# A two-layer hybrid decoder trunk: layer 0's memory heads in three rounded products of split operands with their maps divided on ScalarE, and layer 1's memory values moved to the end of their slot

## The chip, the cores and the metric

The kernel runs on one core of a Trainium2 chip. The metric is the device time of one execution in microseconds (us); the number compared is the median of several runs. A profile of one execution stands beside it: when each instruction of each engine ran, and what it waited for.

## The reference

Two layers over a sequence of 256 tokens with 2048 channels, in float32, with a memory of 256 further rows. Each layer has a mixer and a squared-ReLU MLP; in both mixers 4 heads attend to the memory:

```python
def memory_cross_attention(q, mem, mem_norm_g, w_mem_kv, mq_g, mk_g):
    mkv = rms_norm(mem, mem_norm_g) @ w_mem_kv
    k = mkv[..., :MEM_WIDTH].reshape(B, M, MEM_HEADS, MEM_HEAD_DIM)      # 256 x 4 x 128
    v = mkv[..., MEM_WIDTH:].reshape(B, M, MEM_HEADS, MEM_HEAD_DIM)
    q = rms_norm(q.reshape(B, S, MEM_HEADS, MEM_HEAD_DIM), mq_g)
    k = rms_norm(k, mk_g)
    s = jnp.einsum('bqhd,bkhd->bhqk', q, k).astype(jnp.float32) * (MEM_HEAD_DIM ** -0.5)
    p = jax.nn.softmax(s, axis=-1).astype(v.dtype)
    return jnp.einsum('bhqk,bkhd->bqhd', p, v).reshape(B, S, MEM_WIDTH)

for i in range(2):
    u = rms_norm(x, mix_norm[i]) @ w_in[i]          # columns 1536.. are the memory queries
    # layer 0: causal pooling over windows 2/4/8/16 and per-group maps; layer 1: differential attention
    x = x + concat([token_out, mem_out]) @ w_out[i]
    x = x + squared_relu_mlp(rms_norm(x, ffn_norm[i]), w_ff1[i], w_ff2[i])
```

A head's map `p` is the exponential of the scores divided by its row's sum.

## The kernel before

**Matrices.** A weight comes from memory in blocks of 128x128, 8 to a load (`raw`, or `slab` for the MLP). ScalarE casts a block to a rounded 32-bit type (`F32R`) into `hi_ring` (L166), and VectorE subtracts that from the original and writes the remainder to `lo_ring` (L169). Activations are split in the same way into a high and a low half. A product of two split operands is then three rounded matmuls (high by high, low by high, high by low) that add up in PSUM; the fourth is left out. Both rings have 6 slots of 4 blocks; casts run up to 3 jobs ahead of their use, and a cast can start only when TensorE has finished with the slot it writes.

**Order.** Each engine runs its instructions in the order in which the program holds them. The program is written as a stream of weight blocks; `tick()` is called after every 4 blocks, and `at(d, fn, rank)` puts a piece of other work `d` ticks later. Within one tick the pieces run by rising rank. A scheduler then settles the final order on each engine, from priorities that follow the written order.

**Layer 0.** The memory's keys and values (`wide_step`, L494: TensorE tiles `mk`, `mv`), the memory queries (`mq`), then the pooling projection in tiles `u` (`a_part`, L463 and L465), 16 blocks each. Between these stand the 4 memory heads. `turn_rows` (L616) transposes keys and queries on TensorE (`tr`) and writes them, times a gain, as plain float32. `mem_head` (L656) is called once per head, 4 ticks apart. It holds three pieces:

- `scores`: two float32 matmuls of 128x256 into `ms` (L663), the row maximum `mm_max` on VectorE (L665), two exponentials on ScalarE (L669) into a buffer of 2x256 columns, their sums kept; 2 ticks later `norm`: a reciprocal `mm_rec` (L676) and two multiplications on VectorE (L678).
- `turn`, 4 ticks after the scores: four transposes of 128x128 into `mt` (L686), copied out by ScalarE (L689).
- `pv`, 8 ticks after: two float32 matmuls of 128x256 into `mo` (L694), in the PSUM bank `o`; ScalarE and VectorE write its two halves to `cat` (L695, L696).

Their ranks are 3, 2 and 1: in a tick that holds all three, an older head's `pv` goes first, then the next head's `turn`, then the newest head's `scores`.

**Layer 1.** The same `mem_head` runs for 4 heads beside 12 heads of differential attention. These use the bank `o` too: their values `do` (L1394 to L1396) go there, and VectorE reads them out as `osb` (L1416). The next matmul into the bank, that of a memory head's `pv`, has to wait for this read. Between the pieces run the tiles `mq` (L476 to L478), then `wo` (L463, L465).

Of the kernel before, what the change touches and what calls it, by code (L numbers as in the profile page):

```python
# [14 lines left out]
ALU = mybir.AluOpType  # L15
# [301 lines left out]
def program(ctx, tc, plan, dry, xT, memT, par, lam, cst, wst, yT):  # L317
# [17 lines left out]
    def at(d, fn, rank=0):  # L335
        pend.setdefault(now[0] + d, []).append((rank, fn))
# [71 lines left out]
    def gcol(c):  # L408
        return param[:, c : c + 1]
# [103 lines left out]
    def columns(name):  # L513

        st = stat("tc_" + name)
        for i in range(2):
            nc.tensor.matmul(
                st[:, 2 * i : 2 * i + 2], acc[name][:, i * P : i * P + P], ones_d[:, 0:2],
                start=True, stop=True,
            )  # L520
        v = cp.tile([P, 2], F32, tag="m2", bufs=12, name="cv")
        nc.vector.tensor_scalar_add(v, st[:, 0:4].rearrange("p (a b) -> p a b", b=2)[:, :, 0], EPS)
        col = cp.tile([P, 2], F32, tag="c_" + name, name="c_" + name)
        rsqrt_cols(col, v)
        col2 = cp.tile([P, 2], F32, tag="d_" + name, name="d_" + name)
        nc.vector.tensor_mul(col2, col, col)
        return col, col2


    def key_rows(ps, cols, d):  # L530

        n = 512 // d
        raw = tp.tile([P, 2, 512], F32, tag="rows", bufs=3, name="krow")
        v = vp.tile([P, 2, n], F32, tag="w16", bufs=6, name="kv")
        for t in range(2):
            nc.scalar.activation(raw[:, t, :], ps[t], AF.Copy, scale=cols[0][:, t : t + 1])
            sq = tp.tile([P, 512], F32, tag="rowsq", bufs=1, name="ksq")
            nc.scalar.activation(sq, raw[:, t, :], AF.Square)
            nc.vector.tensor_reduce(
                out=v[:, t, :], in_=sq.rearrange("p (h d) -> p h d", d=d), axis=AX.X, op=ALU.add  # L540
            )
        v = v.rearrange("p t n -> p (t n)")
        nc.vector.tensor_scalar(out=v, in0=v, scalar1=1.0 / d, scalar2=EPS, op0=ALU.mult, op1=ALU.add)
        y = vp.tile([P, 2 * n], F32, tag="w16", bufs=6, name="ky")
        rsqrt_cols(y, v)
        for t in range(2):
            rows = raw[:, t, :].rearrange("p (h d) -> p h d", d=d)
            yb = y[:, t * n : t * n + n].unsqueeze(2).to_broadcast([P, n, d])
            nc.vector.tensor_mul(rows, rows, yb)
        return raw  # L550
# [66 lines left out]
        nc.scalar.activation(dst, turned(raw, i, tag or ("o" if i else "t")), AF.Copy, scale=g)  # L617


    held = {}  # L620

    def mem_query(src, gq, cols):
# [30 lines left out]
        at(2, stats, -2)  # L653
        return q, y

    def mem_head(q, y, k, v, e, pT, out, lag, tag):  # L656

        def scores():  # L660
            s = bk(tag, "ms", (P, 2, T))
            for t in range(2):
                nc.tensor.matmul(s[:, t, :], q[:, t * P : t * P + P], k, start=True, stop=True)  # L663
            m = cp.tile([P, 2], F32, tag="m2", bufs=12, name="mm_max")
            nc.vector.tensor_reduce(out=m, in_=s, axis=AX.X, op=ALU.max, negate=True)  # L665
            nc.vector.tensor_mul(m, m, y)
            z = cp.tile([P, 2], F32, tag="m2", bufs=12, name="mm_sum")
            for t in range(2):
                nc.scalar.activation(  # L669
                    e[:, t, :], s[:, t, :], AF.Exp, bias=m[:, t : t + 1], scale=y[:, t : t + 1],  # L670
                    accum_out=z[:, t : t + 1],
                )

            def norm():
                zr = cp.tile([P, 2], F32, tag="m2", bufs=12, name="mm_rec")
                nc.vector.reciprocal(zr, z)  # L676
                for t in range(2):
                    nc.vector.tensor_scalar_mul(e[:, t, :], e[:, t, :], zr[:, t : t + 1])  # L678

            at(2, norm)  # L680

        def turn():
            t4 = bk("t", "mt", (P, 2, T))
            for mb in range(2):
                for t in range(2):
                    nc.tensor.transpose(  # L686
                        t4[:, mb, t * P : t * P + P], e[:, t, mb * P : mb * P + P], ident
                    )
            nc.scalar.copy(pT, t4)  # L689

        def pv():
            o = bk("o", "mo", (P, T))
            for mb in range(2):
                nc.tensor.matmul(o, v(mb), pT[:, mb, :], start=mb == 0, stop=mb == 1)  # L694
# [47 lines left out]
    def ffn(l, xs, tags, done):  # L742
# [245 lines left out]


    big = sp.tile([P, 4096], F32, tag="big", name="big0")  # L990
    half = sp.tile([P, 2048], F32, tag="half", name="half0")
# [5 lines left out]
    pTb = big[:, 3264:3776].rearrange("p (a t) -> p a t", a=2)  # L997
    mk = half[:, 0:1024].rearrange("p (h t) -> p h t", h=4)
    ebuf = [
        half[:, 1024 + i * 512 : 1536 + i * 512].rearrange("p (a t) -> p a t", a=2) for i in range(2)  # L1000
    ]
    for u in ups:
        nc.vector.memset(u[:, :, 0:16], 0.0)

# [45 lines left out]
            mem_chunk(1)  # L1050
    two_squares("mem", memraw, NK - 2)
    mem_c.extend(columns("mem"))
    mrow = key_rows(kps, mem_c, P)
    for i in range(2):
        at(8, lambda i=i: turn_rows(mrow, 2 * i, mk[:, 2 * i : 2 * i + 2, :], gcol(G_MK)))
# [33 lines left out]
    mq0 = tp.tile([P, 4, T], F32, tag="rows", bufs=3, name="mq0")  # L1089
    for i in range(2):  # L1090
        at(4, lambda i=i: turn_rows(rows0, 2 * i, mq0[:, 2 * i : 2 * i + 2, :], mqg0))
    for h in range(4):
        mem_head(
            mq0[:, h, :], y0.rearrange("p (t h) -> p t h", t=2)[:, :, h], mk[:, h, :],
            lambda mb, h=h: mv[:, mb, h * P : h * P + P], ebuf[h % 2], pTb, cat[:, 12 + h, :],
            6 + 4 * h, f"n{h % 2}",
        )
    pooled = sp.tile([P, 12, 512], F32R, tag="S1", name="pooled")

    def group_u(g):  # L1100
        up = ups[g % 2]
# [464 lines left out]
```

## Time and profile before

| | us |
|---|---|
| median of 3 runs | 2043.78 (2043.53 to 2044.31) |
| the profiled execution's own time | 2045.82 |
| its span, first to last instruction | 2044.0 |
| TensorE busy (matmuls) | 2037.5 |
| VectorE busy | 1665.5 |
| ScalarE busy | 1278.2 |
| mean granted TensorE clock | 1.000 |

In rows of the timeline the first number is the start in us from the first instruction, the second the duration; then the engine (PE is TensorE, PEld its weight loads, DVE VectorE, ACT ScalarE), the line, the operation, the tile written and those read, the shape, and the count of instructions merged. A float32 matmul is recorded as two. Matmuls are pipelined: the next starts before the modelled end of the last, so what a matmul costs on TensorE is read from one start to the next. In the list of waits a row has the sum, the count and the longest, in us.

### The profile page before, as it was taken

What the parts mean: (1) busy time and instruction counts of PE and PEld (TensorE: products, weight loads), DVE (VectorE), ACT (ScalarE), POOL (GpSimd) and SP (SyncE); (2) the same over time, 40 slices, a digit from 0 to 9 for tenths busy, and PEclk for the clock granted to TensorE, in tenths of its full rate; (3) what the DMA queues carried; (4) which work ended last, traced back from release to release, by engine and by line L of the source; (5) the groups of instructions that cost most, each with busy time, mean ns of one, the idle gap of its engine ahead of it and who ended that gap; (6) DMA issues with size and microseconds to landing.
All of it is one profiled execution on the core that took longest, in us unless ns stands there. A gap on an engine that the chain in (4) does not pass through costs nothing.

```text
span 2044.0 us, 30595 instructions
## 1 busy us (share of the span) xinstructions
PE 2037.5 (100%) x11060; PEld 1748.4 (86%) x11060; DVE 1665.5 (81%) x2566; ACT 1278.2 (63%) x2014; POOL 55.2 (3%) x67
## 2 busy tenths in 40 slices
PE   9999999999999999999999999999999999999999
PEld 8888888888888888888888889888888888888888
DVE  7888878878877888899775697878887888887797
ACT  7765566655655655568665697556655655665564
POOL 0001300000000000000000000310000000000000
PEclk9999999999999999999999999999999999999999
DMA  8555555555555555545555544555555555555554
GB/s 305 178 184 188 195 187 193 196 201 190 201 192 194 205 186 189 203 175 199 215 186 192 193 157 139 194 180 192 190 207 195 200 192 191 201 191 197 199 186 145
DMA packets 112616, 393.66 MB, mean 193 GB/s; under 512 B 12816, under 2 KB 15888, under 8 KB 112464
## 3 DMA queue, kind: packets, MB, share of 16 engines
q1 hardware_dynamic: 112320, 391.70, 54.7%
q8 instruction: 86, 1.41, 0.3%
q14 instruction: 66, 0.54, 0.1%
q10 hardware_dynamic: 144, 0.01, 0.0%
HBM read 386.81 MB, written 2.10 MB: 190 GB/s over the span
## 4 chain that ended last, share of the span: by engine, by line
PE 97%; DVE 1%; ACT 1%; issue 0%; DMA 0%; SPq 0%; DVEq 0%; ACTq 0%
PE x_bank L828 32%; PE x_bank L830 16%; PE wo L463 6%; PE p L900 5%; PE p L901 5%; PE p L902 5%; PE k L494 3%; PE v L494 3%; PE ff L828 3%; PE q L494 3%; PE wo L465 3%; PE mk L494 2%; PE u L463 2%; PE mv L494 2%; PE ff L830 2%; PE u L465 1%
## 5 line engine op out<-in xcount | busy, mean ns | idle before, releaser
L166 ACT CAST hi_ring<-raw 128x512 fp32r<-128x512 f32 (+1 forms) x725 | 575.6, 799 | 405.9 <-PE x_bank L828 188.8
L169 DVE TENSOR_TENSOR lo_ring<-raw,hi_ring 128x512 fp32r<-128x512 f32 (+1 forms) x725 | 660.3, 918 | 182.2 <-ACT hi_ring L166 166.3
L828 PE MATMUL x_bank<-fx,hi_ring 128*128 128x512 f32 x1376 | 432.8, 396 | 0.0
L830 PEld LDWEIGHTS x_bank<-fx,lo_ring 128*128 128x128 f32 x1376 | 258.5, 188 | 60.3
L830 PE MATMUL x_bank<-fx,lo_ring 128*128 128x256 f32 x1376 | 270.4, 278 | 0.0
L828 PEld LDWEIGHTS x_bank<-fx,hi_ring 128*128 128x128 f32 x1376 | 215.2, 189 | 10.2 <-ACT room L840 3.7
L169 DVE TENSOR_TENSOR lo_ring<-slab,hi_ring 128x1024 fp32r<-128x1024 f32 (+1 forms) x182 | 187.3, 1032 | 19.9 <-ACT hi_ring L166 19.6
L166 ACT CAST hi_ring<-slab 128x1024 fp32r<-128x1024 f32 (+1 forms) x182 | 163.2, 899 | 47.0 <-PE x_bank L828 39.8
L828 PE MATMUL x_bank<-za,hi_ring 128*128 128x512 f32 x592 | 186.0, 395 | 0.0
L463 PE MATMUL wo<-cat,hi_ring 128*128 128x512 f32 x512 | 162.3, 398 | 0.2 <-DVE resid L733 0.2
L828 PE MATMUL x_bank<-fx,slot 128*128 128x512 f32 x512 | 162.3, 398 | 0.0
L166 ACT CAST slot<-raw 128x1024 fp32r<-128x1024 f32 x84 | 88.2, 1050 | 77.0 <-PE x_bank L828 75.1
L830 PEld LDWEIGHTS x_bank<-za,lo_ring 128*128 128x128 f32 x592 | 111.2, 188 | 26.0
L169 DVE TENSOR_TENSOR slot<-raw,slot 128x1024 fp32r<-128x1024 f32 x84 | 103.0, 1226 | 34.5 <-ACT slot L166 34.5
L169 DVE TENSOR_TENSOR slot<-slab,slot 128x1024 fp32r<-128x1024 f32 x74 | 90.3, 1220 | 42.2 <-ACT slot L166 42.1
L166 ACT CAST slot<-slab 128x1024 fp32r<-128x1024 f32 x74 | 77.9, 1052 | 66.8 <-PE x_bank L828 31.7
L830 PE MATMUL x_bank<-za,lo_ring 128*128 128x256 f32 x592 | 116.3, 278 | 0.0
L830 PEld LDWEIGHTS x_bank<-fx,slot 128*128 128x128 f32 x512 | 96.2, 188 | 22.7
L465 PEld LDWEIGHTS wo<-cat,lo_ring 128*128 128x128 f32 x512 | 96.1, 188 | 21.9
L465 PE MATMUL wo<-cat,lo_ring 128*128 128x256 f32 x512 | 101.7, 278 | 0.0
L830 PE MATMUL x_bank<-fx,slot 128*128 128x256 f32 x512 | 100.6, 278 | 0.0
L828 PEld LDWEIGHTS x_bank<-za,hi_ring 128*128 128x128 f32 x592 | 92.5, 189 | 3.9 <-ACT room L840 0.9
(356 smaller groups left out, 3905.8 us busy)
## 6 DMA issues: line engine op xcount, KB each, us to landing
raw<-in_w SPq DMA_DIRECT2D x596, 512.0 KB, 3.4
slab<-in_w SPq DMA_DIRECT2D x128, 512.0 KB, 3.8
resid<-in_x SPq DMA_DIRECT2D x8, 256.0 KB, 5.8
memraw<-in_mem SPq DMA_DIRECT2D x4, 512.0 KB, 3.8
out_y<-resid SPq DMA_DIRECT2D x16, 128.0 KB, 1.8
memraw<-in_mem SPq DMA_DIRECT2D x6, 256.0 KB, 6.6
qodd<-both SPq DMA_DIRECT2D x6, 256.0 KB, 3.7
qodd<-both SPq DMA_DIRECT2D x6, 128.0 KB, 2.4
```

The source lines that it names most:

```text
L166: cast = self.nc.scalar.copy(hi, src)
L169: self.nc.vector.tensor_sub(lo, src, hi.bitcast(F32))
L463: nc.tensor.matmul(ps, hi, xs[:, k, :], start=first and j == 0, stop=False)
L465: nc.tensor.matmul(ps[:, T : 2 * T], lo, xs[:, k, 0:T], start=False, stop=last and j == len(ks) - 1,)
L494: nc.tensor.matmul(ps[t], a, b, start=i == 0 and j == 0, stop=i == NK - 1 and j == 2)
L828: nc.tensor.matmul(ps, hi, src(k), start=k == ks[0], stop=False)
L830: nc.tensor.matmul(ps[:, T : 2 * T], lo, src(k)[:, 0:T], start=False, stop=k == ks[-1])
L900: nc.tensor.matmul(ps, al, hi[:, s], start=i == 0, stop=False)
L901: nc.tensor.matmul(ps, ah, hi[:, s], start=False, stop=False)
L902: nc.tensor.matmul(ps, ah, lo[:, s], start=False, stop=i == 31)
```

## The change

In layer 0, keys, queries, values and maps are written as a high and a low half: `turn_split` takes the place of `turn_rows`, and the scores and the values become three rounded matmuls each in place of one float32 matmul, so 6 for two in each piece. The low halves lie in space that is free there: those of the queries in `cat`'s rows 14 and 15, those of the values and the maps in rows 12 to 15 of `pooled`, which gets 16 rows and is allocated earlier. One buffer for the exponentials serves all heads, where two took turns. The division of the map moves to ScalarE (`AF.Copy` with a scale per row).

In layer 1 the arithmetic stays. `pv` gets rank 4 and so the last place in its tick, and the transposed maps get two buffers that take turns (`pT1`).

```diff
+    def turn_split(raw, i, dst, g, tag=None):
+        t4 = turned(raw, i, tag or ("o" if i else "t"))
+        nc.scalar.activation(dst[0], t4, AF.Copy, scale=g)
+        stt(dst[1], t4, g, dst[0].bitcast(F32), ALU.mult, ALU.subtract)
...
-    def mem_head(q, y, k, v, e, pT, out, lag, tag):
+    pairs = ((0, 0), (0, 1), (1, 0))
+
+    def mem_head(q, y, k, v, e, pT, out, lag, tag, split=True, pv_rank=1):
+        ab = pairs if split else ((0, 0),)
         def scores():
             s = bk(tag, "ms", (P, 2, T))
             for t in range(2):
-                nc.tensor.matmul(s[:, t, :], q[:, t * P : t * P + P], k, start=True, stop=True)
+                for a, b in ab:
+                    nc.tensor.matmul(
+                        s[:, t, :], q[a][:, t * P : t * P + P], k[b],
+                        start=a + b == 0, stop=(a, b) == ab[-1],
+                    )
...
                 for t in range(2):
-                    nc.vector.tensor_scalar_mul(e[:, t, :], e[:, t, :], zr[:, t : t + 1])
+                    if split:
+                        nc.scalar.activation(
+                            e[:, t, :], e[:, t, :], AF.Copy, scale=zr[:, t : t + 1]
+                        )
+                    else:
+                        nc.vector.tensor_scalar_mul(e[:, t, :], e[:, t, :], zr[:, t : t + 1])
...
-            nc.scalar.copy(pT, t4)
+            nc.scalar.copy(pT[:, 0], t4)
+            if split:
+                nc.vector.tensor_sub(pT[:, 1], t4, pT[:, 0].bitcast(F32))
         def pv():
             o = bk("o", "mo", (P, T))
             for mb in range(2):
-                nc.tensor.matmul(o, v(mb), pT[:, mb, :], start=mb == 0, stop=mb == 1)
+                for a, b in ab:
+                    nc.tensor.matmul(
+                        o, v(mb)[a], pT[:, b, mb, :],
+                        start=mb + a + b == 0, stop=mb == 1 and (a, b) == ab[-1],
+                    )
...
-        at(lag + 8, pv, 1)
+        at(lag + 8, pv, pv_rank)
...
-    mv = tp.tile([P, 2, 512], F32, tag="rows", bufs=3, name="mv0")
+    mv = [tp.tile([P, 2, 512], F32R, tag="rows", bufs=3, name="mv0"), pooled[:, 12:14, :]]
     for t in range(2):
-        nc.scalar.activation(mv[:, t, :], vps[t], AF.Copy, scale=mem_c[0][:, t : t + 1])
+        g = mem_c[0][:, t : t + 1]
+        nc.scalar.activation(mv[0][:, t, :], vps[t], AF.Copy, scale=g)
+        stt(mv[1][:, t, :], vps[t], g, mv[0][:, t, :].bitcast(F32), ALU.mult, ALU.subtract)
...
-    pT1 = carve(512).rearrange("p (a t) -> p a t", a=2)
+    pT1 = [carve(512).rearrange("p (b a t) -> p b a t", b=1, a=2) for _ in range(2)]
...
         mem_head(
-            q, y, mk1[:, h, :], lambda c, h=h: mv1[:, c, h * P : h * P + P],
-            em1, pT1, cat1[:, 12 + h, :], 4, ma,
+            [q], y, [mk1[:, h, :]], lambda c, h=h: [mv1[:, c, h * P : h * P + P]],
+            em1, pT1[h % 2], cat1[:, 12 + h, :], 4, ma, False, 4,
         )
```

How this moves instructions shows at three places. The first is on TensorE, in the slot of layer 0 that holds the values of head 0, the transposes of head 1 and the scores of head 2, between two tiles `u`. Before:

```order
L465 MATMUL u<-xs_122,lo_ring 128x256 x2
L694 MATMUL mo<-big_117,mv_555 128x256 x2
L686 MATMUL mt<-const,half_118 128x128 x4
L663 MATMUL ms<-half_118,mq_827 128x256 x2
L463 MATMUL u<-xs_122,hi_ring 128x512 x2
```

With the change:

```order
L465 MATMUL u<-xs_122,lo_ring 128x256 x2
L715 MATMUL mo<-pooled,mv_556 128x256 x2
L715 MATMUL mo<-pooled 128x256
L715 MATMUL mo<-pooled,mv_556 128x256 x2
L715 MATMUL mo<-pooled 128x256
L704 MATMUL mt<-const,big_117 128x128 x4
L673 MATMUL ms<-half_118,mq_832 128x256 x2
L673 MATMUL ms<-half_118,cat_561 128x256
L673 MATMUL ms<-half_118,mq_832 128x256 x2
L673 MATMUL ms<-half_118,cat_561 128x256
L463 MATMUL u<-xs_122,hi_ring 128x512 x2
```

The pieces keep their places; two instructions became six in each product. The slot before it, with the transposes of head 0 and the scores of head 1, is mixed: one score matmul stands before the first transpose and two more between the first and the second.

The second place is ScalarE's queue in layer 0, from the reciprocal roots of head 0's queries (`rc`) to the exponentials of head 1. Before (L669 the exponentials, L1106 the copy of a `u` tile, L689 the copy of the transposed map):

```order
L428 ACTIVATE rc<-rc,lnc 128x8
L166 CAST hi_ring<-raw_840 128x512 x2
L669 ACTIVATE half_118,mm_sum<-ms,mm_max,qy 128x256 x2
L166 CAST hi_ring<-raw_862 128x512 x2
L1106 COPY u_c<-u 128x256
L166 CAST hi_ring<-raw_901 128x512 x2
L689 COPY big_117<-mt 128x512
L669 ACTIVATE half_118,mm_sum<-ms,mm_max,qy 128x256 x2
```

With the change (L682 the exponentials, L692 the division, L707 the copy of the map; `raw_866` holds the blocks that `raw_862` held):

```order
L428 ACTIVATE rc<-rc,lnc 128x8
L166 CAST hi_ring<-raw_866 128x512 x2
L682 ACTIVATE big_117,mm_sum<-ms,mm_max,qy 128x256 x2
L1137 COPY u_c<-u 128x256
L166 CAST hi_ring<-raw_907 128x512
L692 ACTIVATE big_117<-big_117,mm_rec 128x256 x2
L166 CAST hi_ring<-raw_907 128x512
L707 CAST pooled<-mt 128x512
L166 CAST hi_ring<-raw_942 128x512
L682 ACTIVATE big_117,mm_sum<-ms,mm_max,qy 128x256 x2
```

The two casts that stood behind head 0's exponentials stand before them now, and the division follows a copy and a further cast.

The third place is TensorE in layer 1, the first slot that holds a `pv`, after the last `mq` tile. Before:

```order
L478 MATMUL mq_11184<-x_mx,lo_ring 128x256
L694 MATMUL mo<-att,mv_8666 128x256 x2
L686 MATMUL mt<-const,att 128x128 x4
L663 MATMUL ms<-big_8216,mq 128x256 x2
L463 MATMUL wo<-cat_8669,hi_ring 128x512 x2
```

With the change:

```order
L478 MATMUL mq_11226<-x_mx,lo_ring 128x256
L704 MATMUL mt<-const,att 128x128 x4
L673 MATMUL ms<-big_8258,mq 128x256 x2
L715 MATMUL mo<-att,mv_8708 128x256 x2
L463 MATMUL wo<-cat_8711,hi_ring 128x512 x2
```

The values went from the first place to the last, behind the transposes of head 1 and the scores of head 2. In the next two slots they go behind the transposes (and scores) likewise; the last stands alone in its slot as before.

More of the change, by code (lines that the diff above doesn't have):

```diff
@@ L990, in program @@
     big = sp.tile([P, 4096], F32, tag="big", name="big0")
-    half = sp.tile([P, 2048], F32, tag="half", name="half0")
+    half = sp.tile([P, 2048], F32R, tag="half", name="half0")
     ups = [big[:, i * 816 : i * 816 + 816].rearrange("p (c t) -> p c t", c=3) for i in range(2)]
@@ L996, in program @@
     ]
[L997 to L1001, printed above, removed]
+    ebuf = big[:, 3264:3776].rearrange("p (a t) -> p a t", a=2)
     for u in ups:
@@ L1052, in program @@
     mem_c.extend(columns("mem"))
+    pooled = sp.tile([P, NK, 512], F32R, tag="S1", name="pooled")
     mrow = key_rows(kps, mem_c, P)
+    mk = half.rearrange("p (b h t) -> p b h t", b=2, h=4)
+    mk = [mk[:, b] for b in range(2)]
     for i in range(2):
-        at(8, lambda i=i: turn_rows(mrow, 2 * i, mk[:, 2 * i : 2 * i + 2, :], gcol(G_MK)))
-    mv = tp.tile([P, 2, 512], F32, tag="rows", bufs=3, name="mv0")
+        at(8, lambda i=i: turn_split(mrow, 2 * i, [x[:, 2 * i : 2 * i + 2, :] for x in mk], gcol(G_MK)))
+    mv = [tp.tile([P, 2, 512], F32R, tag="rows", bufs=3, name="mv0"), pooled[:, 12:14, :]]
     for t in range(2):
-        nc.scalar.activation(mv[:, t, :], vps[t], AF.Copy, scale=mem_c[0][:, t : t + 1])
+        g = mem_c[0][:, t : t + 1]
+        nc.scalar.activation(mv[0][:, t, :], vps[t], AF.Copy, scale=g)
+        stt(mv[1][:, t, :], vps[t], g, mv[0][:, t, :].bitcast(F32), ALU.mult, ALU.subtract)
     cat = sp.tile([P, NK, 512], F32R, tag="S0", name="cat0")
@@ L1088, in program @@
     y0 = query_scale(v0, x_c)
-    mq0 = tp.tile([P, 4, T], F32, tag="rows", bufs=3, name="mq0")
+    mq0 = [
+        tp.tile([P, 4, T], F32R, tag="rows", bufs=3, name="mq0"),
+        flat(cat, 14).rearrange("p (h t) -> p h t", h=4),
+    ]
     for i in range(2):
-        at(4, lambda i=i: turn_rows(rows0, 2 * i, mq0[:, 2 * i : 2 * i + 2, :], mqg0))
+        at(
+            4,
+            lambda i=i: turn_split(rows0, 2 * i, [x[:, 2 * i : 2 * i + 2, :] for x in mq0], mqg0),
+        )
+    pTb = flat(pooled, 14).rearrange("p (b a t) -> p b a t", b=2, a=2)
     for h in range(4):
         mem_head(
-            mq0[:, h, :], y0.rearrange("p (t h) -> p t h", t=2)[:, :, h], mk[:, h, :],
-            lambda mb, h=h: mv[:, mb, h * P : h * P + P], ebuf[h % 2], pTb, cat[:, 12 + h, :],
-            6 + 4 * h, f"n{h % 2}",
+            [x[:, h, :] for x in mq0], y0.rearrange("p (t h) -> p t h", t=2)[:, :, h],
+            [x[:, h, :] for x in mk], lambda mb, h=h: [x[:, mb, h * P : h * P + P] for x in mv],
+            ebuf, pTb, cat[:, 12 + h, :], 6 + 4 * h, f"n{h % 2}",
         )
-    pooled = sp.tile([P, 12, 512], F32R, tag="S1", name="pooled")
     def group_u(g):
```

2 lines of the change are left out of this document (added).

## The prediction

> **What bounds the kernel now.** I read the page first, for the engine that sets the end.
>
> ```profile
> span 2044.0 us, 30595 instructions
> PE 2037.5 (100%) x11060; PEld 1748.4 (86%) x11060; DVE 1665.5 (81%) x2566; ACT 1278.2 (63%) x2014; POOL 55.2 (3%) x67
> PE 97%; DVE 1%; ACT 1%; issue 0%; DMA 0%; SPq 0%; DVEq 0%; ACTq 0%
> ```
>
> TensorE is busy through the whole span, and 97% of the chain of work that ended last lies on it. So the time changes only by what TensorE no longer issues, what it issues in addition, and by its waits. How many waits there are to win stands in the list of waits, for TensorE alone, longest in total first:
>
> ```profile
> PE warm L406 <- DVE ones_d L397: 1.1, 1, 1.1
> PE mo L694 <- DVE osb L1416: 0.6, 1, 0.6
> ...
> ```
>
> The first is the start of the program, which the change leaves alone. The second is a memory head's values in layer 1, and the change moves exactly that. No other row is longer, so this kernel has little idle time to give back; the rest must come from cheaper matmuls. That is why I look at three stretches: layer 0's heads, layer 1's slots, and the new work on VectorE and ScalarE that TensorE could come to wait for.
>
> **Part 1: the products of layer 0.** The timeline of TensorE around the slot that holds values, transposes and scores:
>
> ```profile
> 98.88 1.03 PE L694 MATMUL mo<-big,mv 128*128 128x256 f32 x4
> 99.75 0.60 PE L686 MATMUL mt<-const,half 128*128 128x128 f32 x4
> 100.18 1.03 PE L663 MATMUL ms<-half,mq 128*128 128x256 f32 x4
> 100.86 0.80 PE L463 MATMUL u<-xs,hi_ring 128*128 128x512 f32 x2
> 101.50 0.40 PE L465 MATMUL u<-xs,lo_ring 128*128 128x256 f32 x2
> 101.74 0.63 PE L463 MATMUL u<-xs,hi_ring 128*128 128x512 f32 x2
> 102.21 0.39 PE L465 MATMUL u<-xs,lo_ring 128*128 128x256 f32 x2
> ```
>
> The two value matmuls cost 99.75 - 98.88 = 0.87 us. For the scores the row after them must be looked at too: the pair of `u` that follows takes 101.50 - 100.86 = 0.64, where an undisturbed pair takes 102.21 - 101.74 = 0.47. The missing 0.17 is the tail of the scores, so they cost 101.50 - 0.47 - 100.18 = 0.85. What a rounded matmul of 128x256 costs when each has weights of its own is seen in the pooling maps, 27 of them in a row from the first to the second of these:
>
> ```profile
> 118.45 0.28 PE L1138 MATMUL pw<-pooled,hi_ring 128*128 128x256 f32 x1
> ...
> 121.68 0.40 PE L463 MATMUL u<-xs,hi_ring 128*128 128x512 f32 x1
> ```
>
> 3.23 us for 27 is 0.12 each, so six cost 0.72. A head saves (0.87 - 0.72) + (0.85 - 0.72) = 0.28, four heads **1.1 us**. In the slot where the new order mixes transposes with scores, the two extra changes between kinds of matmul may each cost a tail; the only one seen is the 0.17 above. I take 0.1 for both together, between 0 and 0.34.
>
> **Part 2: layer 1's slots.** The first two slots with a `pv`, on TensorE:
>
> ```profile
> 1245.30 0.28 PE L478 MATMUL mq<-x_mx,lo_ring 128*128 128x256 f32 x1
> 1246.23 1.13 PE L694 MATMUL mo<-att,mv 128*128 128x256 f32 x4 [0.65 <-DVE osb L1416]
> 1247.20 0.60 PE L686 MATMUL mt<-const,att 128*128 128x128 f32 x4
> 1247.63 1.03 PE L663 MATMUL ms<-big,mq 128*128 128x256 f32 x4
> 1248.31 0.81 PE L463 MATMUL wo<-cat,hi_ring 128*128 128x512 f32 x2
> 1248.95 0.40 PE L465 MATMUL wo<-cat,lo_ring 128*128 128x256 f32 x2
> ...
> 1256.81 0.27 PE L686 MATMUL mt<-const,att 128*128 128x128 f32 x1
> 1257.20 1.13 PE L694 MATMUL mo<-att,mv 128*128 128x256 f32 x4
> ...
> 1259.83 0.40 PE L465 MATMUL wo<-cat,lo_ring 128*128 128x256 f32 x2
> ```
>
> The last `mq` matmul is over at 1245.30 + 0.12 = 1245.42, the slot at 1248.95 - 0.47 = 1248.48: 3.06 us. Its work is 0.43 for the transposes (1247.63 - 1247.20), 0.85 for the scores and 0.87 for the values, 2.15 in all; 0.91 is waiting and restarting. The second slot runs from 1256.81 to 1259.83 - 0.47 = 1259.36, 2.55 us, and loses 0.40; one transpose had slipped ahead of the wait. What the values wait for is VectorE's read of the shared bank:
>
> ```profile
> 1245.56 0.61 DVE L1416 TENSOR_SCALAR osb<-do,o_y 128x128 f32<-128x128 f32 x2
> 1256.54 0.61 DVE L1416 TENSOR_SCALAR osb<-do,o_y 128x128 f32<-128x128 f32 x2
> ```
>
> These end at 1246.17 and 1257.15. With transposes and scores ahead, TensorE reaches the values at 1245.42 + 1.28 = 1246.70 and at 1256.81 + 1.28 = 1258.09, which is 0.5 and 0.9 after the read: both waits are covered. If that cover failed, the loss would be the part of the 0.91 or 0.40 that sticks out. The transposes do not inherit a wait: in the second slot one already ran first. The third and fourth slots show no such wait in the list, and I give them nothing. Part 2 saves **1.3 us**, at least 0.8 (the first gap alone, 1245.42 to 1246.23), at most 1.4.
>
> **Part 3: the work that is added elsewhere.** What comes on VectorE and ScalarE is sized by the nearest rows:
>
> ```profile
> L361 DVE SCALAR_TENSOR_TENSOR both<-tq,qcol,both 128x512 fp32r<-128x512 f32 x3 | 2.2, 733 | 0.0
> L678 DVE TENSOR_SCALAR half<-half,mm_rec 128x256 f32<-128x256 f32 x8 | 2.4, 348 | 0.1
> L445 ACT ACTIVATE fx<-resid,param 128x256 fp32r<-128x256 f32 x32 | 16.2, 507 | 5.6 <-DVE resid L733 5.6
> L1106 ACT COPY u_c<-u 128x256 f32<-128x256 f32 x12 | 4.4, 369 | 0.8 <-PE u L465 0.8
> ACT hi_ring L166 <- PE u L463: 9.3, 14, 1.4
> ```
>
> VectorE gets six low halves and four subtractions of 128x512, at most 10 x 0.733 = 7.3 us, and loses eight halves of a division, 8 x 0.348 = 2.8. This is hidden by the ring: in that stretch (the list of waits from 60 to 130 us) the casts waited 14 times for TensorE to free a slot, so weights lie ready several blocks ahead, and 4.5 us in pieces of 0.7 do not empty six slots. I cost it at nothing; without that cover it would be the 4.5 itself. The division on ScalarE is another matter, since the transposes wait for it and it stands in a queue. For head 0:
>
> ```profile
> 85.53 0.62 ACT L166 CAST hi_ring<-raw 128x512 fp32r<-128x512 f32 x1 [0.79 <-PE u L463]
> 87.77 0.56 ACT L669 ACTIVATE half<-ms,mm_max,qy 128x256 f32<-128x256 f32 x1 [1.61 <-PE u L463]
> 88.86 1.13 ACT L166 CAST hi_ring<-raw 128x512 fp32r<-128x512 f32 x2
> ...
> 88.99 0.39 PE L465 MATMUL u<-xs,lo_ring 128*128 128x256 f32 x2
> 92.01 0.60 PE L686 MATMUL mt<-const,half 128*128 128x128 f32 x4
> ```
>
> The cast at 85.53 began as TensorE freed a slot; the next two slots come free one and two jobs of four blocks later, after the scores, the second with the end of the pair at 88.99, near 89.22. The two casts that stand now ahead of the exponentials need these slots. So the exponentials start near 89.22 + 0.57 = 89.8 instead of 87.77. They take 88.86 - 87.77 = 1.09, the copy 0.37, the cast 0.57, half the division 0.51: the first half of the map is ready at 92.3, the second at 92.8. TensorE, 0.13 earlier by its faster scores, reaches the first transpose at 92.0 with one score matmul ahead, waits 0.3, and with 0.35 of transpose and scores between waits some 0.15 again: 0.5 for head 0. Behind it wait only TensorE's own next matmuls, so the loss is the wait. For head 2, the tightest of the others by VectorE's load:
>
> ```profile
> 103.50 0.57 ACT L669 ACTIVATE half<-ms,mm_max,qy 128x256 f32<-128x256 f32 x1 [0.47 <-DVE mm_max L666]
> 107.48 0.60 PE L686 MATMUL mt<-const,half 128*128 128x128 f32 x4
> ```
>
> 3.98 us lie between; exponentials, copy, cast and division take 1.09 + 0.37 + 0.57 + 1.01 = 3.04, and the map's subtraction, which VectorE now does ahead of the maximum, 0.73 more. 0.2 remains, about what faster products take from it. I add 0.1 for heads 1 to 3 together: part 3 costs **0.6 us**. From both sides: 0 if the casts find their slots early, 4 x 1.01 = 4.0 if the whole division shows each time.
>
> The Trainium skill speaks against this part: "ScalarE: Activation LUTs", section "Rules for kernel authors", sends multiplications to VectorE, and its section "What ACT_TABLE_LOAD costs" gives 280 ns + 0.833 ns per column with a scale by pointer, by which a half is an estimated 0.49 us and two, overlapping by 0.09, 0.89. The rows agree in direction, 0.507 against 0.348. By the page's figure head 0 would wait 0.1 less; by its rule the division should cost 4 x 0.32 = 1.3 us if nothing hid it, which lies inside the bounds.
>
> **The sum.** -1.1 + 0.1 - 1.3 + 0.6 = **-1.7 us** on a span of 2044.0, so 2042.3. The profiled execution's own time is 2045.82, some 2 us over the median of 2043.78; the change is a difference and carries over: 2042.1. One thing is left at zero with both signs open. The sum of squares moves in TensorE's order:
>
> ```profile
> 73.10 0.39 PE L494 MATMUL mq<-lo_ring,xs 128*128 128x512 f32 x1
> 73.61 0.38 PE L508 MATMUL st_x<-parts,ones_r 128*128 128x256 f32 x1
> ```
>
> From the first to the second row are 0.51 us where such a matmul takes 0.23: a gap of 0.3, which the new place may remove or, with the transposes of the keys beside it, double.
>
> **The rivals.**
>
> *Nothing waits.* The division is hidden and that gap goes: -1.1 - 1.3 - 0.3 = -2.7, so 2041.1. For it: head 0's map is late by 0.3 only, which a slightly earlier slot makes up. Against it: the casts' wait for slots is in the rows.
>
> *The maps come late at every head.* One mechanism: ScalarE's in-order queue holds the division behind a cast that waits for a slot, and the slot comes free only as TensorE nears the transposes. Place: the four transposes `mt` of layer 0. Price: up to 1.01 each, 4.0; the sum is then -1.1 + 0.1 - 1.3 + 4.0 = +1.7, so 2045.5, slower than before. It decides from 2.3 us of waits, about 0.6 a head. Against it: head 2 still has 3.98 us for 3.77 of work.
>
> *The rounded products are bound by their weights.* A weight load takes 1748.4 / 11060 = 0.16 us by the page. If the 48 loads did not overlap with the matmuls, 48 x 0.16 = 7.7 against 4 x 1.72 = 6.9 would be +0.8 instead of -1.1, so 2044.0. Against it: the 27 of 0.12, each with a load of its own.
>
> *The order of layer 1 brings nothing*, because the values wait at their new place as long: -1.1 + 0.1 + 0.6 = -0.4, so 2043.4. Against it: 0.5 and 0.9 of cover.
>
> **How the numbers follow.** The forecast gets 0.55, nothing waits 0.20, late maps 0.13, weights 0.05, no gain in layer 1 0.07. The predicted time is 2042.1; its own range is 2041.3 to 2043.0. To hold 8 in 10, the range takes in the first rival, the last, and half of the late maps: **2040.5 to 2044.5**. 0.2% of the median is 4.1 us, about what a measurement of this kernel can tell from no change. Faster than 2039.7 needs 2.4 us beyond the forecast, more than the bounds hold: 0.08 for what I do not see. Slower than 2047.9 needs late maps at full price and the 4.5 us of VectorE's work uncovered: 0.06. Within it: 0.86.
>
> **What would show it.** In the new profile six `ms` or `mo` matmuls should take 0.72 from first start to the next instruction; 0.9 or more speaks for the weights. TensorE's waits should no longer name `osb`; the slot at 1245 should take 2.15. The waits of `mt` for ScalarE should be the new entry, 0.5 at head 0 and near nothing after; 0.6 or more at each turns the sign. Waits of `u` for `lo_ring` would show that I was wrong to cost VectorE at nothing.

## The result and the profile after

| | before | after |
|---|---|---|
| median of 22 runs each, us | 2044.25 (2043.53 to 2045.38) | 2040.99 (2039.63 to 2042.26) |
| span of the profiled execution, us | 2044.0 | 2039.4 |

The ratio of the medians is 0.9984, with a 95% interval of 0.9978 to 0.9990: 3.26 us less, between 2.0 and 4.5. That is under the 0.2% named in the prediction. The time lies inside its range of 2040.5 to 2044.5, 1.1 below the predicted 2042.1, and nearest to its first rival, nothing waits, with 2041.1. The change itself is nearly twice the forecast of -1.7. The time comes as near as it does partly by luck: the 22 runs put the kernel before 0.47 above the 2043.78 on which the forecast was built, and from 2043.78 the same 3.26 would have led to 2040.52, the edge of the range.

The page of the changed kernel, its span, engines and chain:

```profile
span 2039.4 us, 30621 instructions
PE 2034.0 (100%) x11076; PEld 1746.7 (86%) x11076; DVE 1667.3 (82%) x2568; ACT 1281.1 (63%) x2022; POOL 55.3 (3%) x67
PE 98%; DVE 1%; ACT 0%; DMA 0%; issue 0%; SPq 0%; DVEq 0%; ACTq 0%
```

TensorE still sets the end; its busy time fell by 3.5 us, while VectorE and ScalarE gained 1.8 and 2.9. TensorE's waits in the changed kernel, longest first:

```profile
PE warm L406 <- DVE ones_d L397: 1.1, 1, 1.1
PE p L924 <- ACT hi_ring L166: 0.3, 1, 0.3
PE wo L463 <- DVE resid L757: 0.2, 1, 0.2
...
```

The row of `osb` is gone, and no row of `mt`, `ms` or `u` has come in its place. TensorE's weight loads have a list of their own, and that is where a late map would stand (the run that doubles the division, below, has such a row). From 60 to 165 us, which takes in layer 0's heads, it has two rows in the changed kernel, and neither is a map:

```profile
PEld tr L611 <- DVE krow L549: 0.5, 2, 0.3
PEld st_x L508 <- ACT parts L449: 0.3, 1, 0.3
```

So the division that moved to ScalarE delays nothing that these lists show.

**Where the time went.** Five rows of the timeline cut each execution into stretches: the first `mq` and the first `ms` of layer 0, the first `wo`, the first memory query of layer 1, and the last `mo`. In the kernel before:

```profile
52.12 0.72 PE L494 MATMUL mq<-hi_ring,xs 128*128 128x512 f32 x2
85.56 1.02 PE L663 MATMUL ms<-half,mq 128*128 128x256 f32 x4
162.54 0.40 PE L463 MATMUL wo<-cat,hi_ring 128*128 128x512 f32 x1
1208.29 0.28 PE L476 MATMUL mq<-x_mx,hi_ring 128*128 128x256 f32 x1
1274.77 1.10 PE L694 MATMUL mo<-att,mv 128*128 128x256 f32 x4
```

And in the changed one:

```profile
50.32 0.72 PE L494 MATMUL mq<-hi_ring,xs 128*128 128x512 f32 x2
83.45 0.40 PE L673 MATMUL ms<-half,mq 128*128 128x256 f32 x2
159.34 0.40 PE L463 MATMUL wo<-cat,hi_ring 128*128 128x512 f32 x1
1205.72 0.28 PE L476 MATMUL mq<-x_mx,hi_ring 128*128 128x256 f32 x1
1270.81 1.13 PE L715 MATMUL mo<-att,mv 128*128 128x256 f32 x4
```

The differences between neighbouring rows, and the same for the experiments below (the last column is the rest: from `wo` to layer 1's queries, and from the last `mo` to the end):

| kernel | first `mq` at | `mq` to `ms` | `ms` to `wo` | layer 1 `mq` to `mo` | rest |
|---|---|---|---|---|---|
| before | 52.12 | 33.44 | 76.98 | 66.48 | 1814.98 |
| **after** | 50.32 | 33.13 | 75.89 | 65.09 | 1814.97 |
| layer 1 only | 50.85 | 33.45 | 76.97 | 65.22 | 1814.61 |
| layer 0 only | 50.73 | 33.14 | 75.90 | 66.68 | 1814.75 |
| divide on VectorE | 50.98 | 33.12 | 75.83 | 65.19 | 1816.28 |
| division alone | 50.60 | 33.42 | 76.97 | 66.66 | 1816.35 |
| two products | 50.78 | 33.12 | 74.27 | 65.10 | 1814.13 |
| sums later | 49.99 | 33.54 | 76.98 | 66.51 | 1815.18 |
| one map buffer | 50.92 | 33.14 | 75.88 | 66.93 | 1815.13 |
| double division | 50.97 | 33.13 | 76.19 | 65.34 | 1815.07 |
| both sums later | 50.75 | 33.10 | 76.98 | 66.53 | 1814.44 |
| values between | 50.66 | 33.12 | 75.89 | 65.63 | 1814.20 |
| double low halves | 50.98 | 33.02 | 76.01 | 65.11 | 1814.48 |

The change took 0.31 us from the stretch with the sums of squares, 1.09 from layer 0's heads and 1.39 from layer 1's: **2.79** in all, inside the interval of the medians. The other 1.8 of the two spans' difference of 4.6 lie ahead of the first `mq`. They are not the change's doing: five kernels whose program up to there is that of the kernel before (before, layer 1 only, division alone, and the two with later sums) start it anywhere from 49.99 to 52.12. Where the program is the same, the stretches of layer 0 repeat within some 0.1 us and that of layer 1 within 0.25 (66.48 to 66.68 with the old order, 65.09 to 65.34 with the new), one execution each. That is far finer than the medians of the experiments, whose intervals are about 1.8 us wide on either side. So the experiments are read mostly by stretches.

### The profile page after: what moved, and what is told of

The parts are those of the page before. It is cut to its first block, busy times and chain, and to the rows that moved or that the text cites. A ratio compares the mean times of both kernels' runs of the same rounds, so it can differ in the third digit from the quotient of the medians.

```text
span 2039.4 us, 30621 instructions
## 1 busy us (share of the span) xinstructions
PE 2034.0 (100%) x11076; PEld 1746.7 (86%) x11076; DVE 1667.3 (82%) x2568; ACT 1281.1 (63%) x2022; POOL 55.3 (3%) x67
## 4 chain that ended last, share of the span: by engine, by line
PE 98%; DVE 1%; ACT 0%; DMA 0%; issue 0%; SPq 0%; DVEq 0%; ACTq 0%
PE x_bank L852 32%; PE x_bank L854 16%; PE wo L463 6%; PE p L924 5%; PE p L925 5%; PE p L926 5%; PE k L494 3%; PE v L494 3%; PE ff L852 3%; PE q L494 3%; PE wo L465 3%; PE u L463 2%; PE mk L494 2%; PE mv L494 2%; PE ff L854 2%; PE u L465 1%
```

## The experiments

The theory of terms has the gain add up from three independent pieces (products, gap, layer 1's order), with the division and VectorE's new work hidden. Each run was timed beside the kernel before; its difference is against that median.

**Layer 1 alone and layer 0 alone.** The first is the kernel before with layer 1's two lines changed (`mem_head` takes the rank as an argument):

```diff
-    pT1 = carve(512).rearrange("p (a t) -> p a t", a=2)
+    pT1 = [carve(512).rearrange("p (a t) -> p a t", a=2) for _ in range(2)]
...
-            em1, pT1, cat1[:, 12 + h, :], 4, ma,
+            em1, pT1[h % 2], cat1[:, 12 + h, :], 4, ma, 4,
```

> The kernel before with layer 1's part alone: the values last in their slot (rank 4) and two buffers for the transposed maps; layer 0 as before. Theory of terms: the two waits for osb go, 0.91 + 0.40 = 1.3 us, so 2044.25 - 1.3 = 2043.0, the first slot takes 2.15 us from the last mq matmul to wo. Rival, the order of layer 1 brings nothing and the gain of the change lies elsewhere: 2044.25, a slot of 3.06. In both the first mq of layer 0 starts where it does in the kernel before (52.1).

The second is the change without that:

```diff
-    pT1 = [carve(512).rearrange("p (b a t) -> p b a t", b=1, a=2) for _ in range(2)]
+    pT1 = [carve(512).rearrange("p (b a t) -> p b a t", b=1, a=2) for _ in range(1)]
...
-            em1, pT1[h % 2], cat1[:, 12 + h, :], 4, ma, False, 4,
+            em1, pT1[0], cat1[:, 12 + h, :], 4, ma, False, 1,
```

> The change without layer 1's part: rank 1 and one buffer there, layer 0 as changed. Theory of terms: products -1.1, the gap before the sum of squares -0.3, division nothing: 2044.25 - 1.4 = 2042.85, with the two waits for osb back. Rival, the start: the 1.8 us by which the first mq of layer 0 begins earlier in the changed kernel (50.3 against 52.1) come from the change (where its buffers lie), and then the time is 2044.25 - 1.4 - 1.8 = 2041.05 and the first mq begins near 50.3 again; if they are a matter of the single execution, the first mq begins anywhere between 50 and 53.

Measured beside 2044.74: layer 1 alone 2043.37 (-1.37, ratio 0.9995, interval 0.9986 to 1.0004), layer 0 alone 2043.08 (-1.66, 0.9992, 0.9983 to 1.0001). Neither difference is certain by itself, but together they give 3.03, near the 3.26 of the whole. The stretches are sharper: layer 1 alone shortens only its own (66.48 to 65.22), layer 0 alone only its two, by 0.30 and 1.08, where the whole change has 0.31 and 1.09. The rival of the start falls: layer 1 alone, without any edit ahead of it, starts its first `mq` at 50.85, layer 0 alone at 50.73. (That layer 1 alone would start at 52.1 was expected, and missed.) In layer 0 alone the wait for `osb` is back:

```profile
PE mo L715 <- DVE osb L1447: 0.7, 1, 0.7
```

**The engine of the division.** First the change with the division of layer 0 back on VectorE, then the reverse edit, the kernel before with layer 0's division on ScalarE and nothing else:

```diff
-                    if split:
-                        nc.scalar.activation(
-                            e[:, t, :], e[:, t, :], AF.Copy, scale=zr[:, t : t + 1]
-                        )
-                    else:
-                        nc.vector.tensor_scalar_mul(e[:, t, :], e[:, t, :], zr[:, t : t + 1])
+                    nc.vector.tensor_scalar_mul(e[:, t, :], e[:, t, :], zr[:, t : t + 1])
```

> The change, but with the maps of layer 0 divided on VectorE as before (two multiplications of 0.35 us instead of two on ScalarE of 0.41 and 0.51). Theory of terms: the division is hidden on either engine, 2041.0 within 0.3. Rival, the division on ScalarE costs the 0.6 us of the prediction's part 3: 2040.4. Second rival, the move to ScalarE is what keeps VectorE free, which has 4.5 us of low halves more: waits of mt for VectorE, up to 0.5 a head, 2041.5 to 2043.

> The kernel before with the division of layer 0's maps on ScalarE, nothing else. Theory of terms: hidden, 2044.25 within 0.3, no wait of mt for ScalarE over 0.1. Rival, ScalarE's queue delays the maps (the cast ahead of the division waits for a slot): 0.1 to 0.5 us of wait per head at mt, 2044.7 to 2046.2.

Measured 2041.84 (-2.90, 0.9986, 0.9977 to 0.9995) and 2045.01 (+0.27, 1.0000, 0.9991 to 1.0009). By themselves both times would fit the rivals that have the maps wait (2041.5 to 2043 and 2044.7 to 2046.2), but the stretches do not, and in neither kernel do the two lists, of TensorE and of its weight loads, name a map from 60 to 165 us. Layer 0's heads take 75.83 in the first against 75.89 in the changed kernel, and 76.97 in the second against 76.98: the move of the division is worth less than 0.1 on either side. In this case a multiplication may stand on ScalarE, against "Rules for kernel authors" in the Trainium skill's "ScalarE: Activation LUTs", because nothing on the path waits for it.

In one place the first is shorter by more than that 0.06. There the scheduler left the transposes of head 0 and the scores of head 1 unmixed. That slot, from its first row to the next `u`:

```profile
90.39 0.60 PE L699 MATMUL mt<-const,big 128*128 128x128 f32 x4
...
91.54 0.63 PE L463 MATMUL u<-xs,hi_ring 128*128 128x512 f32 x2
```

It takes 1.15 us. In the changed kernel the same work is mixed and takes 91.01 - 89.73 = 1.28, so 0.13 more; the later slots give 0.07 of that back, most of it in head 3's values (0.70 in the changed kernel against 0.76):

```profile
89.73 0.28 PE L673 MATMUL ms<-half,mq 128*128 128x256 f32 x1
89.88 0.33 PE L704 MATMUL mt<-const,big 128*128 128x128 f32 x1
89.96 0.36 PE L673 MATMUL ms<-half,mq 128*128 128x256 f32 x1
90.16 0.28 PE L673 MATMUL ms<-half,cat 128*128 128x256 f32 x1
90.28 0.54 PE L704 MATMUL mt<-const,big 128*128 128x128 f32 x3
90.58 0.48 PE L673 MATMUL ms<-half,mq 128*128 128x256 f32 x2
90.90 0.28 PE L673 MATMUL ms<-half,cat 128*128 128x256 f32 x1
91.01 0.63 PE L463 MATMUL u<-xs,hi_ring 128*128 128x512 f32 x2
```

**Two products instead of three.** The product of one operand's low half goes:

```diff
-    pairs = ((0, 0), (0, 1), (1, 0))
+    pairs = ((0, 0), (1, 0))
```

> The change with two products in place of three in layer 0's heads; left out are high queries by low keys, and high values by the low half of the maps. 16 rounded matmuls fewer. Theory of terms: 0.12 each, so 1.9 us less than the changed kernel, 2039.1; four ms in 0.47 from the first start to the next instruction, and the stretch from the first ms to the first pw 1.9 shorter than the 31.95 of the changed kernel. Rival, such matmuls are bound by their weight loads (0.16 by the page): 2.6 less, six ms would have cost 0.96 and the products nothing. Second rival, the products' gain is hidden behind the maps: nothing changes, 2041.0.

Measured 2038.95 beside 2043.85 (-4.90, 0.9977, 0.9968 to 0.9986). Layer 0's heads fall by 1.62 to 74.27, where 1.92 was expected: 0.10 for a matmul instead of 0.12. Its first scores, and the transposes and scores of the slot that holds head 2's scores:

```profile
83.90 0.28 PE L673 MATMUL ms<-half,mq 128*128 128x256 f32 x1
...
84.38 0.62 PE L463 MATMUL u<-xs,hi_ring 128*128 128x512 f32 x2
...
97.08 0.62 PE L704 MATMUL mt<-const,big 128*128 128x128 f32 x4
97.46 0.36 PE L673 MATMUL ms<-half,mq 128*128 128x256 f32 x1
97.67 0.28 PE L673 MATMUL ms<-half,cat 128*128 128x256 f32 x1
97.78 0.28 PE L673 MATMUL ms<-half,mq 128*128 128x256 f32 x1
```

Four undisturbed matmuls take 0.48, so 0.12 each is right, and the rival of the weights (0.16 each, 2.6 less) falls. The shortfall of 0.3 lies mostly in one slot. The slot shown here, from head 0's values to the next `u`, falls by 0.45 of the 0.48 expected (1.86 to 1.41). The next one, with head 3's scores, this kernel mixes and the changed kernel does not; it falls by 0.30 only (1.86 to 1.56). One price of mixing is the change of kind: the first rounded matmul behind float32 transposes takes 97.67 - 97.46 = 0.21 to the next, and in a mixed slot this comes twice. The rest of the 0.3 is spread over the other slots, at most 0.06 in each. It is the fastest kernel of the study, but it drops low-order terms that the changed kernel keeps.

**The gap before the sums.** The kernel before with `st_x` written later, which the whole change had done only through the scheduler; then with the column sums `tc_x` moved too:

```diff
         if k == 12:
-            x_r.append(rstd_from("x"))
             x_c.extend(columns("x"))
+            at(4, lambda: x_r.append(rstd_from("x")))
```

> The kernel before with the two matmuls of the sum of squares (st_x) written four ticks later, so that they stand together between the last mq and the first u; nothing else is changed. Theory of terms: the gap of 0.3 ahead of st_x goes, the stretch from the first mq to the first ms is 33.1 to 33.2 in place of 33.5, 0.3 to 0.4 us less than the kernel before. Rival, the gap is not a wait that moving cures (the sums still come late or a restart costs the same in the new place): 33.5, same time as before.

```diff
         if k == 12:
-            x_r.append(rstd_from("x"))
-            x_c.extend(columns("x"))
+            at(4, lambda: (x_r.append(rstd_from("x")), x_c.extend(columns("x"))))
```

> The kernel before with both readers of the finished sum of squares (st_x and the column sums tc_x) written four ticks later; the run with st_x alone moved left the wait in place, at tc_x. Theory of terms: with no early reader the gap goes, the stretch from the first mq to the first ms takes 33.1 to 33.2 us in place of 33.44, as in the changed kernel (33.13), and layer 0's heads stay at 76.98 from the first ms to the first wo. Rival, the 0.3 of the changed kernel come from its other edits in that stretch (keys and queries written as halves) and not from the order of the sums: 33.4 to 33.6.

The first missed: 33.54, and 2043.76 against 2043.85. `st_x`, which reads the sum `acc` through its split `parts`, no longer waits there. But the scheduler drew `tc_x` forward (71.0, where the kernel before has it at 77.8); it now comes first to the same sum and waits in its stead:

```profile
70.48 0.39 PE L494 MATMUL mq<-hi_ring,xs 128*128 128x512 f32 x1
71.04 0.58 PE L517 MATMUL tc_x<-ones_d,acc 128*128 128x2 f32 x4 [0.17 <-DVE acc L1026]
```

From 70.48 to 71.04 are 0.56 where one such matmul takes 0.23, so the gap is 0.33, as large as before. With both moved the stretch is 33.10, 0.34 shorter, and the two matmuls of `st_x` run without a gap (0.23 together):

```profile
73.31 0.40 PE L508 MATMUL st_x<-parts,ones_r 128*128 128x256 f32 x2
73.54 0.62 PE L463 MATMUL u<-xs,hi_ring 128*128 128x512 f32 x2
```

So the 0.31 of the whole change is this gap: the first reader of the finished sum must stand late enough, whichever it is. The median (2043.89 against 2044.13) is too coarse to show it.

**One buffer for layer 1's maps.** The change with one buffer for all heads:

```diff
-    pT1 = [carve(512).rearrange("p (b a t) -> p b a t", b=1, a=2) for _ in range(2)]
+    pT1 = [carve(512).rearrange("p (b a t) -> p b a t", b=1, a=2) for _ in range(1)]
...
-            em1, pT1[h % 2], cat1[:, 12 + h, :], 4, ma, False, 4,
+            em1, pT1[0], cat1[:, 12 + h, :], 4, ma, False, 4,
```

Here the next head's map overwrites the one that the values still need, so the values of three heads are computed with the wrong map; the time is that of the waits alone.

> The change with a single buffer for the transposed maps in layer 1; the values still last in their slot. Theory of terms: TensorE does not need the second buffer, since the copy of the next map has a slot's time to finish: 2041.0 within 0.3, slots of 2.15. Rival, ScalarE's copy of the next map now waits for the values (mo) and holds the casts behind it: ScalarE waits some 1 us in two slots, and if the ring doesn't cover it, 2041.5 to 2043, with waits of wo for hi_ring.

Measured 2042.91 (-0.94, 0.9996, 0.9987 to 1.0005); layer 1's stretch is 66.93, longer than the 66.48 of the kernel before. The time lies where the rival put it, but none of the expectations saw why: the values do not wait for room, they wait for the copy that has just been issued.

```profile
1246.09 1.13 PE L715 MATMUL mo<-att,mv 128*128 128x256 f32 x4 [0.83 <-ACT att L707]
```

The second buffer is thus a part of the reordering, not an addition to it.

**Doubling what was costed at nothing.** First a copy in place behind each half of ScalarE's division:

```diff
                             e[:, t, :], e[:, t, :], AF.Copy, scale=zr[:, t : t + 1]
                         )
+                        nc.scalar.activation(e[:, t, :], e[:, t, :], AF.Copy)
```

> The change with each half of the division followed by a copy of the same size in place on ScalarE (0.92 us more per head, 3.7 in all). It measures the cover of the division. The trace of the changed kernel leaves a slack between the map's end and its transposes of some 0.1 at head 0, 1.4, 0.9 and 0.2 at heads 1 to 3; in this kernel the scores of head 1 stand ahead of the transposes of head 0, 0.6 of further cover there. Theory of terms: waits of mt for ScalarE of 0.3 at head 0, 0.7 at head 3, near nothing between: 1.0 us over the changed kernel, 2042.0. Rival, the slack is larger than the rows show (the whole of it is hidden): 2041.0. Rival, all of it shows at every head: 2044.7.

Measured 2041.08 (-2.77, 0.9987, 0.9978 to 0.9996); layer 0's heads take 76.19, 0.30 more than in the changed kernel. The copies are cheaper than I wrote:

```profile
89.95 0.92 ACT L692 ACTIVATE big<-big,mm_rec 128x256 f32<-128x256 f32 x2
90.77 0.71 ACT L695 ACTIVATE big<-big 128x256 f32<-128x256 f32 x2
91.38 0.61 ACT L166 CAST hi_ring<-raw 128x512 fp32r<-128x512 f32 x1
```

From start to start two divisions hold the queue for 0.82, two copies for 0.61. The Trainium skill, "ScalarE: Activation LUTs", section "What ACT_TABLE_LOAD costs", gives 186 ns + 0.833 ns per column, 93 ns more for each operand by pointer, and an overlap of 93 ns; the estimates are 0.80 and 0.61, close to these rows. So 2.44 us were added to ScalarE in place of the 3.7 expected, and 0.30 of it came out on TensorE: between hidden altogether and the 1.0 of my theory. Now the list of the weight loads names the maps:

```profile
PEld mt L705 <- ACT big L695: 0.4, 2, 0.3
```

The two are 0.17 at head 0 and 0.26 at head 2, where heads 0 and 3 were expected. Their slots are longer by 0.07 and 0.18, and the last 0.05 lie in head 3's values; the orders on ScalarE and TensorE changed a little besides. TensorE's own list stays empty there, so it is the weight loads' list that tells a late map. In the changed kernel this row is missing: the division is hidden, with some room.

Then VectorE's ten new low halves and subtractions computed twice, in `turn_split`, for the values, and here for the maps:

```diff
-            if split:
+            for _ in range(2 if split else 0):
                 nc.vector.tensor_sub(pT[:, 1], t4, pT[:, 0].bitcast(F32))
```

> The change with each of its ten new low halves and subtractions of layer 0 computed twice on VectorE (some 7 us more there). Theory of terms: VectorE's new work is covered by the ring and by the time between pieces; doubled, it still costs at most 0.2 us: 33.1 to 33.3 from the first mq to the first ms and 75.9 to 76.1 from the first ms to the first wo. Rival, VectorE was only just free: waits of u for lo_ring or of mo for the low halves of the maps, up to 0.7 a head, 3 us in all.

Measured 2040.97 beside 2044.13 (-3.16, 0.9983, 0.9974 to 0.9993), with 33.02 and 76.01: 0.01 more than the changed kernel over both stretches. That is a net figure, as the orders moved: the first stretch is 0.11 shorter, the mixed slot of head 1's scores 0.10, while the slot with head 3's transposes is 0.23 longer, where a weight load of `mt` now waits 0.26 for ScalarE's division. No row of either list has TensorE wait for VectorE in layer 0's heads, so VectorE had room there for twice the work.

**The values of layer 1 in the middle.** Rank 2.5 in place of 4, so transposes, values, scores:

```diff
-            em1, pT1[h % 2], cat1[:, 12 + h, :], 4, ma, False, 4,
+            em1, pT1[h % 2], cat1[:, 12 + h, :], 4, ma, False, 2.5,
```

> The change with layer 1's values between transposes and scores (rank 2.5) in place of last. By the rows of the kernel before, the read of osb ends 0.75 us after the last mq matmul in the first slot and 0.34 after the start of the second; TensorE now reaches the values 0.43 after. Theory of terms (cover against read): a wait of 0.3 in the first slot, none in the second; the stretch from the first mq of layer 1's heads to the last mo takes 65.4 in place of 65.1, and osb stands in TensorE's list with 0.2 to 0.4. Rival, what helps is that the values are not first, whatever stands ahead: 65.1 and no osb. Rival, the values need the whole of transposes and scores ahead: 66.0 or more.

Measured 2041.55 (-2.58, 0.9988, 0.9978 to 0.9998); the stretch is 65.63, 0.5 over that of the change. The first slot:

```profile
1242.57 0.60 PE L704 MATMUL mt<-const,att 128*128 128x128 f32 x4
1243.38 1.13 PE L715 MATMUL mo<-att,mv 128*128 128x256 f32 x4 [0.21 <-DVE osb L1447]
```

The transposes take 0.43, so the values could run at 1243.00 and start at 1243.38: a loss of 0.38, 0.21 of it named as a wait, where the two rows of the kernel before gave 0.3. VectorE's read ends at 1242.71 + 0.61 = 1243.32 here. It is the work ahead against the end of the read, and not the mere change of place. The two rivals (nothing lost, 0.9 or more lost) fall.

## Why the prediction was right, and where it was wrong

**Part 1, the products: right.** The six rounded `ms` of head 0 run from 83.45 to the next `u` at 84.16, 0.71 where 0.72 was said. Layer 0's heads gave 1.09 for a sum of -1.1 + 0.1. The 0.1 for the mixed slot was of the right size: its 1.28 against 1.15 unmixed (with the division on VectorE). By the four passes of true float32 that the Trainium skill's "FP8 and Floating Point Precision", section "TensorE Precision Notes", states, three products would cost three quarters of 0.85, an estimated 0.64; the rows say 0.71, and they decide.

**Part 2, layer 1: right.** The first slot with a `pv` of the changed kernel, TensorE and then VectorE's read:

```profile
1242.74 0.28 PE L478 MATMUL mq<-x_mx,lo_ring 128*128 128x256 f32 x1
1242.86 0.60 PE L704 MATMUL mt<-const,att 128*128 128x128 f32 x4
1243.30 1.03 PE L673 MATMUL ms<-big,mq 128*128 128x256 f32 x4
1244.16 1.03 PE L715 MATMUL mo<-att,mv 128*128 128x256 f32 x4
1244.84 0.81 PE L463 MATMUL wo<-cat,hi_ring 128*128 128x512 f32 x2
1245.49 0.40 PE L465 MATMUL wo<-cat,lo_ring 128*128 128x256 f32 x2
```

```profile
1243.00 0.61 DVE L1447 TENSOR_SCALAR osb<-do,o_y 128x128 f32<-128x128 f32 x2
```

From 1242.86 to 1245.49 - 0.47 are 2.16, predicted 2.15. The read ends at 1243.61, and TensorE comes to the values 0.55 later, predicted 0.5. The stretch fell by 1.39, with layer 1 alone by 1.26; the term was 1.3. The second slot takes 2.17 where it took 2.55.

**Part 3, the division: the step that failed** is "waits 0.3, and with 0.35 of transpose and scores between waits some 0.15 again: 0.5 for head 0", and with it the 0.1 for heads 1 to 3. No such wait is in the changed kernel. ScalarE's queue around head 0 in the changed kernel:

```profile
86.91 0.62 ACT L166 CAST hi_ring<-raw 128x512 fp32r<-128x512 f32 x1 [0.77 <-PE u L463]
87.44 0.56 ACT L682 ACTIVATE big<-ms,mm_max,qy 128x256 f32<-128x256 f32 x1
...
88.53 0.36 ACT L1137 COPY u_c<-u 128x256 f32<-128x256 f32 x1
88.78 0.63 ACT L166 CAST hi_ring<-raw 128x512 fp32r<-128x512 f32 x1
89.30 0.92 ACT L692 ACTIVATE big<-big,mm_rec 128x256 f32<-128x256 f32 x2
```

The prediction's times, moved by the 2.11 between the two first `ms` and by the 0.14 of faster scores, are 86.97 for the second cast, 87.55 for the exponentials, and 90.05 and 90.55 for the halves of the map. The order, the wait for the slot and the place of the first transpose (89.9 by that scale, 89.88 measured) were right. Two errors went the same way. The prediction gave the 0.13 of faster scores to the transposes but not to the slots, though these come free behind the same scores: the pair whose end frees the second slot starts 3.26 after the first `ms` in the changed kernel and 3.43 in the kernel before. And the queue was summed too long: I added full durations where the next instruction starts before the last has ended. The copy holds the queue for 0.25 and not 0.37, the cast for 0.52 and not 0.57, and the second half of the division comes 0.41 after the first, not 0.51. So the pair ends at 89.30 + 0.92 = 90.22, 0.33 earlier than said, and the three other transposes at 90.28 (in the mixed slot above) find it there by 0.06. Together the two errors, 0.33 and 0.14, come to nearly all of the 0.5 that was said.

**VectorE costed at nothing: right**, and with room: doubling its new work added 0.01 net.

**The gap left at zero with both signs open** came out at -0.31, as the first rival had it. With that and part 3 at nothing, the prediction's own terms give -1.1 + 0.1 - 1.3 - 0.3 = -2.6, for 2.79 in the stretches and 3.26 in the medians. Between these two I can't say more: the difference lies inside the interval.

**The rivals.** Nothing waits (2041.1) is what happened. Late maps fell by the two lists of waits and by both runs on the division's engine; bound by weights fell by the 0.71 and the 0.48; no gain in layer 1 fell by the 1.26 of layer 1 alone.

## What to carry to other kernels

A queue of short instructions is summed from start to start, not by recorded durations; where the margin is smaller than that error, both outcomes belong in the range with like chances. A wait is moved off the path by putting ahead of it work as long as the wait's end is late, and no less: 0.43 of transposes covered part of a read, 1.28 with the scores all of it. When the first reader of a value is moved, look who reads it next, since the wait can go there. A late operand may show only in the list of the weight loads.

## What the runs showed of the hardware

Rounded matmuls of 128x256 behind float32 transposes cost 0.09 us more at the change of kind (0.21 against 0.12), so mixing pieces on TensorE has a price even without a wait. Before the first `mq` and in the rest of the kernel, single executions of like programs differ by some 2 us (first `mq` from 49.99 to 52.12, the rest from 1814.1 to 1816.4), while the stretches around the change repeat within 0.1 to 0.25; why is open.
